# Layer 0's gate strips of six heads in pairs, by seven block products, ahead of attention 0

## The chip, the cores and the metric

One core of one Trainium2 chip runs the whole program in one launch. The metric is the device time of that core in microseconds (us), as the median over executions; lower is better. The engines are TensorE (PE, with its weight loads shown as PEld), VectorE (DVE), ScalarE (ACT), GpSimd (POOL) and SyncE (SP), which issues all the DMAs of this kernel.

## The reference, cut to what matters

A trunk of two layers on 1024 tokens of width 1024, all in float32. Each layer normalizes, applies a shift and a scale that come from a vector `c`, mixes the tokens, multiplies by a SiLU gate and projects back. Layer 0 is differential attention with eight heads; layer 1 is latent attention.

```python
def _diff_attention(h, positions, w_in, ...):
    proj = h @ w_in
    q, k, v, z = jnp.split(proj, [DA_WIDTH, 2 * DA_WIDTH, 3 * DA_WIDTH], axis=-1)
    q = _rope(q.reshape(b, s, 2 * DA_HEADS, DA_QK_DIM), positions)
    k = _rope(k.reshape(b, s, 2 * DA_HEADS, DA_QK_DIM), positions)
    ...
    def block(qb):
        sc = jnp.einsum('bqhcd,bkhcd->bhcqk', qb, k, preferred_element_type=f32) * scale
        p = jax.nn.softmax(sc, axis=-1)
        p = p[:, :, 0] - lam * p[:, :, 1]
        return jnp.einsum('bhqk,bkhd->bqhd', p.astype(v.dtype), v)
    o = _from_blocks(lax.map(block, _to_blocks(q)))
    o = _rmsnorm(o, subln_g) * (1.0 - lambda_init)
    o = o.reshape(b, s, DA_WIDTH) * jax.nn.silu(z)
    return o @ w_out
```

The change is about `z`, the gate: `h` (1024 x 1024) times the last 1024 columns of `w_in`. A head owns 128 of those columns; that is its gate strip.

## The kernel before, in words

**Numbers in two halves.** Every float32 operand of a matmul is split into a high part of PE's reduced format and the remainder. ACT writes the high part (a cast), POOL or DVE subtracts it from the raw value. `mm3` (L171 to L175) then makes a product of three matmuls: high by high, high by low, low by high. A strip (`strip0`, two raw tiles of 128x512 through `fetch_strip` and `split_raw`, L218 and L219) by 512 tokens is eight such products, 24 matmuls of 128x512; a whole strip is 48.

**Stages of layer 0, as PE runs them.** First the normalized, modulated and transposed tokens `h0[k][half]` are made (`h_chunk`) while the values of the heads 0 to 3 and part of the first key strip are multiplied. Then come the second halves of head 0's key and query strips (the `gen_half` loops ahead of `st1.close()`), then a stream of strips, of which `stream0.step(Z_PRE)` runs the first 16 steps (head 0's gate strip). A step is one `mm3`. Then `v0_tile` makes the values of heads 4 to 7, with weights `wv1`, and after that attention 0 runs head by head (`attn0`).

**Attention 0.** A head has eight query tiles. `q_tile` computes two score blocks per tile (c = 0 and 1, L866), each followed by a maximum on DVE (L412) and an exponential on ACT (L414); DVE combines both (L872 to L874). There are two score buffers in PSUM, so the second scores of a tile wait for the combination of the tile before. `after_scores` transposes the combined tile (L395), splits it (L397 on ACT, L398 on DVE) and, at every second tile, multiplies two tiles with the values (`pv`). Between these pieces the stream of strips is stepped: `FILL0` says how many steps at each of six places of a tile. Head by head the stream makes the key, query and gate strips of the next one. `side` is a list of small jobs (rotation and stacking of keys and queries), of which every step starts one.

**The order.** The program is traced in the order of the code; a planner then fixes each engine's order from its own costs: when an engine is free, it takes what is ready, earlier code first. `tc.issue_after(x)` puts a block's instructions behind x on x's engine; `in_turn` keeps program order. Buffers are named by pool and tag, with a fixed number each; a pool that is closed gives its space to the next one opened on the same side, and a new tile waits for the old tiles that lay there.

**Layer 1** already makes the gates of its heads 2 to 7 in pairs. `combos` forms sums and differences of the token blocks, `z_weights` those of the weight blocks, and `z_pair` combines seven products (`zacc` in the profile, L1801 to L1837); the finished gates go through DRAM (`zS`).

Of the kernel before, what the change touches and what calls it, by code (L numbers as in the profile page):

```python
# [21 lines left out]
P = 128  # L22
# [4 lines left out]
HF = 512  # L27
# [49 lines left out]
def f32v(ap):  # L77
    return ap.bitcast(F32)
# [3 lines left out]
def trunk(ctx: ExitStack, tc: tile.TileContext, A, out):  # L82
# [240 lines left out]

    def rope(rp, acc, half, scale, eng=G, add=V):

        cs = slice(half * HF, half * HF + HF)
        raw = rp.tile([P, HF], F32, name="rp_raw", tag="rp", bufs=6)
        sw = rp.tile([P, HF], F32, name="rp_sw", tag="rp", bufs=6)
        r = rp.tile([P, HF], F32, name="rp_r", tag="rp", bufs=6)
        if scale == 1.0:  # L330
# [212 lines left out]
    def load_wv(src, eng=G):  # L543
        return split_wv(fetch_wv(src), eng)
# [223 lines left out]
    def k_done(h):  # L768
        def f(acc, half):
            rot, fin = rope(wp, acc, half, 1.0, *[G if h else V] * 2)  # L770

# [10 lines left out]
    def q_done(h):  # L782
        def f(acc, half):
            rot, fin = rope(wp, acc, half, SC0, *[G if h else V] * 2)

# [24 lines left out]
    def strip0(kind, h):  # L810
        return lambda: fetch_strip([A["w_s0"][kind, h, f] for f in range(2)], [4, 4])

    items = []
    for h in range(NH):
        items += [(strip0(1, h), h0, k_done(h)), (strip0(0, h), h0, q_done(h)), (strip0(2, h), h0, z_done(h))]
    wv1 = [load_wv(A["w_v0"][k, 1], V) for k in range(WV1)]
    with tc.issue_after(mod_load.last):
        z0raw = fetch_strip([A["w_s0"][2, 0, f] for f in range(2)], [4, 4])
    with tc.issue_after(store_v.act):
        wv1 += [load_wv(A["w_v0"][k, 1], V) for k in range(WV1, KT)]  # L820
    with tc.issue_after(h_last):
        k_done(0)(kacc, 0)
    for _ in gen_half(wk0, h0, 1, lambda acc: k_done(0)(acc, 1)):
        pass
    wz0 = split_strip(z0raw)
    q_done(0)(qacc, 0)
    for _ in gen_half(wq0, h0, 1, lambda acc: q_done(0)(acc, 1)):
        pass
# [6 lines left out]
    stream0 = Stream(gen_strips(items[2:], [wz0]))  # L835
    lam4 = p1b.tile([P, 4, 64], F32, name="lam4", tag="lam", bufs=1)
    with tc.issue_after(mod_load.last):
        SP.dma_start(lam4, A["lam"].to_broadcast([P, 4, 64]))
    lp = sm.tile([P, 2], F32, name="lp")
# [38 lines left out]
    for tt in range(8):  # L878
# [6 lines left out]
        for t in pend[2 + 2 * tt : 4 + 2 * tt] if tt else ():  # L885
            with tc.issue_after(silu_gate.last):
                t()
# [268 lines left out]
    def gate_step0():  # L1156
        nonlocal slot0
        next(gate0, None)
        slot0 += 1

    for h in range(NH - 1):
        attn0(h, lambda i: FILL0[i], lambda i: gate_step0())
    class Seven:
# [627 lines left out]

    def gate_out(h, half, c_, dst):

        th = wst.tile([P, HF], F32, name="zth", tag="gz", bufs=3)
        S.activation(th, c_, AF.Tanh, scale=0.5)
        V.scalar_tensor_tensor(out=dst, in0=th, scalar=1.0, in1=c_, op0=ALU.add, op1=ALU.mult)
        SP.dma_start(zS[h, half], dst)

    zw = z_weights()
# [10 lines left out]
    def z_pair(p, late=lambda i: None):  # L1810
# [5 lines left out]
        V.tensor_add(c_, acc, u)  # L1816
        gate_out(2 * p, 0, c_, c_)
        V.tensor_add(u, product(TC[2]), u)
# [10 lines left out]
        V.tensor_add(u, acc, u)  # L1829
        gate_out(2 * p + 1, 1, c_, c_)  # L1830
# [4 lines left out]
        gate_out(2 * p + 1, 0, u3, u3)  # L1835
        V.tensor_add(u, product(h1q(1, 1)), u)
        gate_out(2 * p, 1, u, u)  # L1837

# [590 lines left out]
```

## Time and profile before

| what | us |
|---|---|
| median of three runs | 1400.3 |
| lowest and highest | 1397.07 and 1401.43 |
| the profiled execution's own time | 1398.53 |
| its span, first to last instruction | 1396.8 |
| PE busy | 1368.8 |
| DVE busy | 932.6 |
| ACT busy | 740.7 |
| POOL busy | 756.6 |
| mean granted clock of PE | 0.997 |

Busy times are of one profiled execution. Matmuls are pipelined, so the busy time of one (about 0.39 us for 128x512) is longer than the step from its start to the next one's.

### The profile page before, as it was taken

To read this page: it belongs to the slowest core of one execution; us is meant where nothing else is said; L and a number is where in the kernel's file an instruction comes from. 1 tells how busy PE (TensorE), PEld (TensorE's weight loads), DVE (VectorE), ACT (ScalarE), POOL (GpSimd) and SP (SyncE) were. 2 spreads that over 40 slices of the span, in tenths; PEclk is the share of its full clock that TensorE was granted. 3 is DMA by queue.
4 is the path that set the end of the run, shared out by engine and by line. 5 is a ranking of instruction groups with operands and counts; after the bars stand their busy time and mean duration, and the time that the engine had idled before them with its cause. 6 is when DMAs were issued, how large, how long until landed. Compare 5 with 4: busy or idle time off the path is not lost.

```text
span 1396.8 us, 20691 instructions
## 1 busy us (share of the span) xinstructions
PE 1368.8 (98%) x7334; PEld 1146.1 (82%) x7334; DVE 932.6 (67%) x1311; ACT 740.7 (53%) x1338; POOL 756.6 (54%) x592
## 2 busy tenths in 40 slices
PE   9999999999999999999999999999999999999997
PEld 6787888888888888887887888888888888888886
DVE  7654787777666666668596985645656555555684
ACT  5532465656555556566647552335454554545554
POOL 5434374758686858675794143532141273844673
PEclk9999999999999999999999999999999999999999
DMA  9857644343444434526555246399433364576463
GB/s 340 264 177 243 189 119 139 103 144 100 150 125 149 127 120 124 157 58 207 197 206 175 57 130 214 125 296 279 131 98 120 106 196 136 194 226 216 141 247 121
DMA packets 149386, 232.06 MB, mean 166 GB/s; under 512 B 20641, under 2 KB 57633, under 8 KB 149282
## 3 DMA queue, kind: packets, MB, share of 16 engines
q1 hardware_dynamic: 149282, 230.74, 52.2%
q8 instruction: 58, 0.95, 0.3%
q14 instruction: 46, 0.38, 0.1%
HBM read 144.74 MB, written 61.81 MB: 148 GB/s over the span
## 4 chain that ended last, share of the span: by engine, by line
PE 77%; DVE 7%; POOL 4%; DMA 4%; ACT 3%; issue 3%; SPq 1%; POOLq 0%; ACTq 0%; DVEq 0%
PE s L2043 10%; PE acc L173 8%; PE acc L175 8%; PE acc L174 8%; PE tr L395 7%; PE s L866 7%; PE pv L173 4%; PE pv L175 4%; PE pv L174 4%; DMA ada<-in_ada_ss 2%; PE oy L174 1%; PE oy L175 1%; PE oy L173 1%; DVE ada L436 1%; PE zacc L175 1%
## 5 line engine op out<-in xcount | busy, mean ns | idle before, releaser
L397 ACT CAST pth<-tr 128x512 fp32r<-128x512 f32 x256 | 150.3, 587 | 285.8 <-PE tr L395 281.2
L412 DVE TENSOR_REDUCE nm<-s 128x1 f32<-128x1024 f32 x192 | 234.0, 1219 | 78.7 <-PE s L866 70.5
L398 DVE TENSOR_TENSOR ptl<-tr,pth 128x512 fp32r<-128x512 f32 x256 | 176.3, 689 | 150.7 <-ACT pth L397 146.2
L219 POOL TENSOR_TENSOR wl<-wraw,wh 128x512 fp32r<-128x512 f32 (+2 forms) x77 | 102.3, 1330 | 211.9 <-ACT wh L218 168.8
L414 ACT ACTIVATE e<-s,nm 128x1024 f32<-128x1024 f32 x128 | 143.7, 1122 | 35.2 <-DVE nm L412 34.9
L395 PE MATMUL tr<-ident,e 128*128 128x128 f32 x1024 | 155.2, 274 | 4.0 <-DVE ptl L398 3.8
L395 PEld LDWEIGHTS tr<-ident,e 128*128 128x128 f32 x1024 | 120.7, 140 | 46.7 <-DVE ptl L398 24.5
L173 PE MATMUL acc<-h0h,wh 128*128 128x512 f32 x360 | 150.1, 417 | 0.0
L173 PE MATMUL pv<-pth,vt 128*128 128x256 f32 x512 | 147.6, 288 | 0.0
L174 PE MATMUL pv<-ptl,vt 128*128 128x256 f32 x512 | 145.5, 284 | 0.0
L175 PE MATMUL pv<-pth,vt 128*128 128x256 f32 x512 | 144.6, 282 | 0.0
L175 PE MATMUL acc<-h0h,wl 128*128 128x512 f32 x360 | 141.6, 393 | 0.0
L174 PE MATMUL acc<-h0l,wh 128*128 128x512 f32 x360 | 141.1, 392 | 0.0
L336 POOL TENSOR_TENSOR rp_r<-rp_raw,cosT 128x512 f32<-128x512 f32 x36 | 47.1, 1308 | 106.6 <-ACT rp_raw L333 53.2
L173 PEld LDWEIGHTS pv<-pth,vt 128*128 128x128 f32 x512 | 97.2, 190 | 2.9 <-ACT pth L397 0.2
L174 PEld LDWEIGHTS pv<-ptl,vt 128*128 128x128 f32 x512 | 97.4, 190 | 2.4
L175 PEld LDWEIGHTS pv<-pth,vt 128*128 128x128 f32 x512 | 97.3, 190 | 0.0
L1199 POOL TENSOR_TENSOR wol<-wol,woh 128x512 fp32r<-128x512 f32 x56 | 82.9, 1503 | 25.5 <-ACT woh L1198 23.9
L866 PE MATMUL s<-ks,qa 128*128 128x512 f32 x256 | 82.8, 404 | 4.2 <-DVE e L874 3.2
L874 DVE SCALAR_TENSOR_TENSOR e<-s,z,e 128x1024 f32<-128x1024 f32 x64 | 82.2, 1284 | 2.2
L866 PE MATMUL s<-ks,qb 128*128 128x512 f32 x256 | 79.9, 393 | 0.5 <-DMA qb<-qb 0.5
L175 PEld LDWEIGHTS acc<-h0h,wl 128*128 128x128 f32 x360 | 67.6, 188 | 15.0
(421 smaller groups left out, 3467.2 us busy)
## 6 DMA issues: line engine op xcount, KB each, us to landing
ada<-in_ada_ss SPq DMA_DIRECT2D x32, 512.0 KB, 5.7
wraw<-in_w_s SPq DMA_DIRECT2D x64, 256.0 KB, 2.8
vS<-v_hl SPq DMA_DIRECT2D x32, 512.0 KB, 5.7
vt<-vS SPq DMA_DIRECT2D x32, 512.0 KB, 4.8
wol<-tS SPq DMA_DIRECT2D x56, 256.0 KB, 5.3
tS<-ob SPq DMA_DIRECT2D x48, 256.0 KB, 2.0
rp_sw<-rp_raw SPq DMA_DIRECT2D x160, 64.0 KB, 2.0
bc_s<-bc_d SPq DMA_DIRECT2D x34, 256.0 KB, 3.9
```

The lines of the kernel that those rows point to most:

```text
L173: PE.matmul(psum, ah, bh, start=first, stop=False, skip_group_check=skip)
L174: PE.matmul(psum, ah, bl, start=False, stop=False, skip_group_check=skip)
L175: mm3.last = PE.matmul(psum, al, bh, start=False, stop=last, skip_group_check=skip).ins
L219: sub = (V if pair_of else G).tensor_sub(l_[:, :n], raw[:, :n], f32v(h_[:, :n]))
L395: transpose_p.last = PE.transpose(tr[:, j, :], p[:, kt * P : (kt + 1) * P], ident).ins
L397: mk["S"] = S.copy(pth[kh][:, :, dst], tr).ins
L398: mk["V"] = V.tensor_sub(ptl[kh][:, :, dst], tr, f32v(pth[kh][:, :, dst])).ins
L412: mk["V"] = V.reduce_max(nm, s_ps, axis=AX.X, negate=True).ins
L414: mk["S"] = S.activation(e, s_ps, AF.Exp, bias=nm, scale=1.0, accum_out=zs).ins
L866: PE.matmul(s_ps[:, kc * HF : (kc + 1) * HF], src[:, c, ql], KS[h][kc][:, c, :], start=fst, stop=not fst)
L1199: sub = eng.tensor_sub(lo, raw, f32v(hi))
L2043: PE.matmul(s_ps[:, kc * HF : (kc + 1) * HF], lhs, rhs(kc), start=i == 0, stop=i == 4)
```

## The change

Gate strips of layer 0's heads 0 to 5 are no longer made in attention 0's stream. They are made ahead of it, in three pairs. For a pair the two strips form a 2 x 2 block of weights (head by upper and lower half of the width, 512 rows each), the tokens a 2 x 2 block (width half by token half), and seven products of blocks, each four `mm3`, take the place of eight. Four of the seven take combinations of token blocks as their moving operand (`TK[1]` to `TK[4]`, made once by `combos0`, 17 jobs in `side`), and five take combinations of weight blocks (`z0_weights`). Head 6's gate strip is made whole ahead of the pairs, head 7's stays in the stream. All gates but head 7's are written to `zS` in DRAM and read back by `load_gates` at the second tile of their head.

To make room, the pools of the first stage (`p1a`, `p1b`) are closed earlier; the combinations live in their space (`zp` on the left, `tp` on the right). Head 0's keys and queries are written to DRAM as they come out of PSUM (`park`, `rS`) and are rotated later, from there. The query weights `wq0` move to pool `pg`. The value weights `wv1` are all loaded and split after the pairs. Head 1's key strip takes the 16 steps that head 0's gate strip had ahead of `v0_tile`. `FILL0` goes from 47 steps a head to 31, `Z_LAST` from 2 to 1.

The diff, cut to its core:

```diff
-FILL0 = ((1, 2, 1, 1, 1, 0), (1, 1, 1, 1, 1, 1)) * 3 + ((1, 2, 1, 1, 1, 0), (1, 1, 1, 1, 1, 0))
+FILL0 = ((1, 1, 1, 1, 1, 0), (1, 0, 1, 0, 1, 0)) * 3 + ((1, 1, 1, 1, 1, 0), (1, 0, 1, 0, 0, 0))
-Z_LAST = 2
-FILL7 = ((0, 1, 2, 1, 1, 0),) + ((0, 1, 1, 1, 1, 0),) * 2
+Z_LAST = 1
+Z_PAIRS = 3
+FILL7 = ((0, 1, 1, 1, 1, 0), (0, 1, 1, 1, 0, 0))
...
+    rS = dr.tile([2, 2, P, HF], F32, name="rS")
...
-    def rope(rp, acc, half, scale, eng=G, add=V):
+    def rope(rp, acc, half, scale, eng=G, add=V, parked=None):
...
+        src = raw if parked is None else parked
+        if parked is not None:
+            SP.dma_start(raw, parked)
...
-            SP.dma_start(sw[q * 32 : q * 32 + 32], raw[(q ^ 1) * 32 : (q ^ 1) * 32 + 32])
+            SP.dma_start(sw[q * 32 : q * 32 + 32], src[(q ^ 1) * 32 : (q ^ 1) * 32 + 32])
...
-        t = p1.tile([P, 2, HF], F32R, name="wq0", tag="ada", bufs=ADA_B)
+        t = pg.tile([P, 2, HF], F32R, name="wq0", tag="ada", bufs=2)
...
-        items += [(strip0(1, h), h0, k_done(h)), (strip0(0, h), h0, q_done(h)), (strip0(2, h), h0, z_done(h))]
-    wv1 = [load_wv(A["w_v0"][k, 1], V) for k in range(WV1)]
+        items += [(strip0(1, h), h0, k_done(h)), (strip0(0, h), h0, q_done(h))]
+    items.append((strip0(2, NH - 1), h0, z_done(NH - 1)))
...
+    def park(kind, scale):
+        def f(acc, half):
+            t = wp.tile([P, HF], F32, name="rp_park", tag="rp", bufs=6)
...
+            SP.dma_start(rS[kind, half], t)
+        return f
+
+    def gate_out(h, half, c_):
+
+        th = wst.tile([P, HF], F32, name="zth", tag="gz", bufs=3)
+        S.activation(th, c_, AF.Tanh, scale=0.5)
+        V.scalar_tensor_tensor(out=c_, in0=th, scalar=1.0, in1=c_, op0=ALU.add, op1=ALU.mult)
+        SP.dma_start(zS[h, half], c_)
...
     st1.close()
+    st1b.close()
+    stZ, stT0 = ExitStack(), ExitStack()
+    zp = pool(stZ, "zp")
+    tp = pool(stT0, "tp", side="right")
...
+    def combos0():
+        todo_ = []
+        def split_t():
+            n, k, t = todo_.pop(0)
+            hi, lo = TK[n][k] = [tp.tile([P, HF], F32R, name=f"t{n}{k}{x_}") for x_ in "hl"]
+            S.copy(hi, t)
+            V.tensor_sub(lo, t, f32v(hi))
+        def later(*job):
+            if todo_:
+                split_t()
+            todo_.append(job)
+        for k in range(4):
+            (ah, al), (bh, bl), (ch, cl), (dh, dl) = [[f32v(x_) for x_ in h0[k + 4 * q][half]] for half in range(2) for q in range(2)]
+            c_, d_, t1, t2, t3, t4 = [zt(x_) for x_ in ("tc", "td", "t1f", "t2f", "t3f", "t4f")]
+            V.tensor_add(c_, ch, cl)
+            V.tensor_sub(t1, c_, ah)
+            V.tensor_sub(t1, t1, al)
+            later(1, k, t1)
+            yield
+            V.tensor_add(d_, dh, dl)
+            V.tensor_sub(t2, d_, t1)
+            later(2, k, t2)
+            yield
+            V.tensor_sub(t4, bh, t2)
+            V.tensor_add(t4, t4, bl)
+            later(4, k, t4)
+            yield
+            V.tensor_sub(t3, d_, c_)
+            later(3, k, t3)
+            yield
+        split_t()
+        yield
+    def z0_weights():
+        for _ in range(Z_PAIRS):
+            a11, a12 = zraw[:2]
+            yield split_raw(a11, 4)
+            yield split_raw(a12, 4)
...
+            V.tensor_add(s1, a21, a22)
+            V.tensor_sub(a21, a11, a21)
+            V.tensor_sub(a11, s1, a11)
+            V.tensor_sub(a12, a12, a11)
+            for t in (a12, a11, s1, a21, a22):
+                yield split_raw(t, 4)
+    def product0(rhs):
+        hi, lo = zq.pop(0)
+        zq.append(next(zw, None))
+        acc = bank("acc", "zacc")
+        for k in range(4):
+            mm3(acc, hi[k], lo[k], *rhs[k], k == 0, k == 3)
+            side.tick()
+        return acc
+    def z0_pair(p):
+        u = rpt0("zu")
+        S.copy(u, product0(h0q(0, 0)))
+        c_ = rpt0("z11")
+        V.tensor_add(c_, product0(h0q(1, 0)), u)
+        gate_out(2 * p, 0, c_)
+        v = rpt0("zv")
+        S.copy(v, product0(h0q(1, 1)))
...
+        V.tensor_add(u, product0(TK[2]), u)
+        u5 = rpt0("zu5")
+        V.tensor_add(u5, product0(TK[1]), u)
+        V.tensor_add(v, v, u5)
+        gate_out(2 * p, 1, v)
...
+        acc = product0(TK[3])
+        V.tensor_add(u5, acc, u5)
+        V.tensor_add(u, acc, u)
+        gate_out(2 * p + 1, 1, u5)
+        V.tensor_add(u, product0(TK[4]), u)
+        gate_out(2 * p + 1, 0, u)
+    z0_fetch(0, ((0, 0), (0, 1), (1, 0), (1, 1)))
+    cg = combos0()
+    for _ in range(17):
+        side.add(lambda: next(cg), None)
+    for _ in gen_half(wk0, h0, 1, lambda acc: park(1, 1.0)(acc, 1)):
+        side.tick()
+    wz6 = split_strip(z6raw)
+    for _ in gen_half(wq0, h0, 1, lambda acc: park(0, SC0)(acc, 1)):
+        side.tick()
+    zw = z0_weights()
+    zq = [next(zw)]
+    for half in range(2):
...
+        for _ in gen_half(wz6, h0, half, put):
+            side.tick()
+    zq.append(next(zw))
+    for p in range(Z_PAIRS):
+        if p == Z_PAIRS - 1:
+            k1raw = fetch_strip([A["w_s0"][1, 1, f] for f in range(2)], [4, 4])
+        z0_pair(p)
+    stT0.close()
+    stZ.close()
...
+    wk1 = split_strip(k1raw)
+    for half in range(2):
+        k_done(0)(None, half, rS[1, half])
+    wv1 = [load_wv(A["w_v0"][k, 1], V) for k in range(KT)]
+    for half in range(2):
+        q_done(0)(None, half, rS[0, half])
+    stream0 = Stream(gen_strips(items[2:], [wk1]))
...
+    def beside0(h, i):
+        if i == 1:
+            load_gates(h)
+        gate_step0()
```

More of the change, by code (lines that the diff above doesn't have):

```diff
@@ L817, in trunk, with h0q @@
+    def gate_out(h, half, c_):
[3 more added lines that the diff above has]
+        SP.dma_start(zS[h, half], c_)
+    def h0q(q, half):
+        return [h0[4 * q + k][half] for k in range(4)]
     with tc.issue_after(mod_load.last):
[L818 to L820 removed]
+        z6raw = fetch_strip([A["w_s0"][2, NH - 2, f] for f in range(2)], [4, 4])
@@ L821, in trunk @@
     with tc.issue_after(h_last):
[L822 to L828, printed above, removed]
-    st1.close()
+        park(1, 1.0)(kacc, 0)
+    park(0, SC0)(qacc, 0)
+    st1.close()
+    st1b.close()
+    stZ, stT0 = ExitStack(), ExitStack()
+    zp = pool(stZ, "zp")
+    tp = pool(stT0, "tp", side="right")
+    TK = {n: [None] * 4 for n in range(1, 5)}
@@ new lines, in trunk, with z0_fetch, zt @@
+    zraw = []
+    def z0_fetch(p, parts):
+        for m, f in parts:
+            raw = zp.tile([P, HF], F32, name="zraw", tag="zraw", bufs=8)
+            SP.dma_start(raw, A["w_s0"][2, 2 * p + m, f])
+            zraw.append(raw)
+    def zt(name):
+        return zp.tile([P, HF], F32, name=name, tag="zt", bufs=8)
+    def combos0():
[30 more added lines that the diff above has]
+        yield
@@ L830, in trunk @@
+    zq.append(next(zw))
+    k1raw = None
+    for p in range(Z_PAIRS):
+        if p == Z_PAIRS - 1:
+            k1raw = fetch_strip([A["w_s0"][1, 1, f] for f in range(2)], [4, 4])
+        z0_pair(p)
+    assert not side.q and next(zw, None) is None
+    stT0.close()
+    stZ.close()
+    st1b = ExitStack()
+    p1b = pool(st1b, "p1c", side="right")
     st2a = ExitStack()
@@ L885, in trunk @@
         for t in pend[2 + 2 * tt : 4 + 2 * tt] if tt else ():
-            with tc.issue_after(silu_gate.last):
+            with tc.issue_after(split_wv.last):
                 t()
```

51 lines of the change are left out of this document (33 added, 18 removed).

## The prediction

> **What bounds the kernel now.** I read the page's head and chain first, then busy time by window, then single instructions around the places that the change touches.
>
> ```profile
> span 1396.8 us, 20691 instructions
> PE 1368.8 (98%) x7334; PEld 1146.1 (82%) x7334; DVE 932.6 (67%) x1311; ACT 740.7 (53%) x1338; POOL 756.6 (54%) x592
> PE 77%; DVE 7%; POOL 4%; DMA 4%; ACT 3%; issue 3%; SPq 1%; POOLq 0%; ACTq 0%; DVEq 0%
> ```
>
> PE is busy 98% of the span and 77% of the chain of waits runs through it. A matmul taken out is time won, unless another engine becomes late. By window (PE, PEld, DVE, ACT, POOL busy, granted clock, DMA share, GB/s):
>
> ```profile
> 81.20:92.20 11.00, 10.94 (x48) 9.08 (x49) 4.57 (x7) 3.45 (x7) 2.59 (x2) 1.00 0.95 275
> 92.20:103.10 10.90, 10.90 (x50) 9.03 (x49) 7.00 (x11) 4.45 (x8) 4.41 (x4) 1.00 0.42 118
> 148.00:640.00 492.00, 487.34 (x2716) 412.19 (x2715) 352.18 (x496) 290.19 (x514) 337.94 (x273) 1.00 0.43 127
> 859.00:916.90 57.90, 57.51 (x255) 47.29 (x254) 38.01 (x50) 21.01 (x37) 31.23 (x24) 1.00 0.53 175
> ```
>
> From 81.2 to 103.1 PE makes the second halves of head 0's key and query strips and then its gate strip, without a gap, while DVE has 11.6 of 21.9 us of work, most of it splits of `wv1` that move away. Attention 0 (148 to 640) is dense too. The window at 859 is layer 1's pair loop: the same seven products three times, also dense.
>
> **What is won.** Each pair saves one block product of 12 matmuls: 36 in all. Their pitch:
>
> ```profile
> 92.27 0.39 PE L173 MATMUL acc<-h0h,wh 128*128 128x512 f32 x1
> 103.15 0.39 PE L173 MATMUL vps<-wvh,h0h 128*128 128x512 f32 x1
> 859.07 0.39 PE L173 MATMUL zacc<-h_h,wh 128*128 128x512 f32 x1
> 916.88 0.39 PE L173 MATMUL vps<-wvh,ckh 128*128 128x512 f32 x1
> ```
>
> 48 matmuls take 10.88, so 0.227 each; 252 (three pairs of 84) take 57.81, or 0.229. 36 x 0.227 = **-8.2**. The rest only moves: 348 matmuls go ahead of `v0_tile` (48 + 3 x 84 + 48 for head 1's keys, in place of head 0's 48), 112 steps leave the seven heads.
>
> **The combined tokens and weights.** The new DVE work ahead of the first pair is 48 additions and subtractions of 128x512 (per k eight sums and four low parts). Four weight sums follow, and two gate multiplications of head 6 fall between. Their pitch is shown by layer 1's own combinations:
>
> ```profile
> 802.78 0.69 DVE L1628 TENSOR_TENSOR t4f<-h_h,t2f 128x512 f32<-128x512 f32 x1
> 807.60 0.69 DVE L1628 TENSOR_TENSOR t2f<-h1f,t1f 128x512 f32<-128x512 f32 x1
> 808.32 1.66 DVE L1628 TENSOR_TENSOR t4f<-h_h,t2f 128x512 f32<-128x512 f32 x1
> 807.41 2.02 POOL L219 TENSOR_TENSOR wl<-wraw,wh 128x512 fp32r<-128x512 f32 x1 [7.72 <-ACT wh L218]
> ```
>
> Eight instructions lie between the first two rows: 4.82/8 = 0.60 each. 48 take 29.0, well over the 21.9 of PE work that covers them.
>
> When can they start? The `zt` tiles lie where `p1a` was, and the values that wait for their store lay there last:
>
> ```profile
> 80.52 2.48 DVE L375 TENSOR_TENSOR v_hl<-vacc,v_hl 128x512 fp32r<-128x512 f32 x4
> 81.23 4.25 SPq L377 DMA_DIRECT2D vS<-v_hl  x4
> DMA to landing us min/median/max: 3.7/5.7/8.4
> ```
>
> The last stores go out between 81.2 and 85.5 and land 3.7 to 8.4 later. The earliest lands at 85, the last issued later; some buffers are free before others. I take 86.0; the limits are 83.0 (DVE's end of these values, if the space in question held others) and 87.
>
> When are they due? PE, dense, ends the key and query halves at 92.3 and head 6's strip at 103.15; the products follow each 12 x 0.227 = 2.73 apart: second 105.9, third 108.6, fourth 111.3. The third needs `a12'`, which is the last of the four weight sums. In code these sums are traced only when the first product is called, behind 47 of the 48 combinations (`side` puts an empty entry behind each job, so one job goes per two steps), and the planner takes earlier code first. Path: 86.0 + 29.0 = 115.0, + 2 gates and 4 sums at 0.6 = 118.6, then the split:
>
> ```profile
> L218 ACT CAST wh<-zraw 128x512 fp32r<-128x512 f32 x18 | 10.9, 618 | 16.6 <-PE zacc L174 9.7 <-DVE zraw L1787 3.6 <-POOL wl L219 1.5
> L219 POOL TENSOR_TENSOR wl<-zraw,wh 128x512 fp32r<-128x512 f32 x18 | 24.6, 1374 | 32.9 <-ACT wh L218 29.6 <-DVE zraw L1787 3.2
> ```
>
> 0.62 + 1.30 (the unhindered subtraction) = 120.5. The low part is first read at the third product's third matmul, 108.6 + 0.45 = 109.05. **+11.5** of PE idle. By then the fourth product's tokens are ready, and the later products' weights come from the same sums, two casts and subtractions per 2.73 us; nothing more is late in pair 1. In pairs 2 and 3 the layer 1 window, dense with the same work, says the weights are in time.
>
> The bounds of this term: with the start at 83.0 and the weights planned first, the last combination that the fourth product needs is ready at 83.0 + 46 x 0.604 + 2.4 = 113.2, due at 113.4 (its fourth k): **0**. With the start at 87 and three collisions like 808.32 (1.66 against 0.69, so 1.0 each): **15.6**. I take the middle of these paths, since the 80.52 and 81.23 rows put the start near 86 and nothing in the code puts the weights earlier.
>
> The Trainium skill, page "SBUF — State Buffer", section "Who interferes with whom", says that a VectorE instruction with both inputs in SBUF contends with a GpSimd instruction that reads SBUF, and that the loser waits. The 808.32 and 807.41 rows agree. By it all of the subtractions for head 6's strip and the first weights, some three in the window, would cost 1.0 each: the sum would be 3 higher. I keep them in the bound alone.
>
> **The clock behind the stall.** A long idle of PE lowered its granted clock at the head of layer 1:
>
> ```profile
> 767.08 0.33 PE L484 MATMUL trh<-ident,x 128*128 128x128 f32 x1 [2.85 <-DVE x L473]
> 760.00:770.00 10.00, 7.15 (x31) 5.46 (x30) 6.57 (x9) 5.36 (x9) 4.81 (x4) 0.89 0.30 102
> 770.00:780.00 10.00, 10.00 (x52) 8.22 (x52) 8.74 (x12) 5.27 (x9) 0.00 (x0) 0.94 0.07 16
> ```
>
> 0.11 x 10 + 0.06 x 10 = **+1.7**, once; 0 without the stall.
>
> **Attention 0 with less to fill.** Each tile pair loses four steps of stream. Between the second scores of a tile and the combination that frees the buffer runs a chain on DVE and ACT (columns as above: start, duration):
>
> ```profile
> 311.76 0.62 PE L866 MATMUL s<-ks,qa 128*128 128x512 f32 x2
> 316.24 1.28 DVE L874 SCALAR_TENSOR_TENSOR e<-s,z,e 128x1024 f32<-128x1024 f32 x1
> 317.93 0.62 PE L866 MATMUL s<-ks,qa 128*128 128x512 f32 x2
> 336.18 0.73 PE L866 MATMUL s<-ks,qa 128*128 128x512 f32 x2 [0.55 <-DVE e L874]
> ```
>
> The chain is 317.52 - 311.76 = 5.76, PE's own work over the same path 6.17. One step less (3 x 0.23 = 0.69) makes 5.48: short by 0.28. The pair at 336.18, where DVE also does the normalization's row, waits already (0.55) and would be short by up to 0.68 more. With 28 pairs, 14 of each kind, nothing moved: 14 x 0.27 + 14 x 0.68 = 13.3. But the planner draws matmuls of the stream forward when the scores aren't ready:
>
> ```profile
> 282.77 1.28 DVE L874 SCALAR_TENSOR_TENSOR e<-s,z,e 128x1024 f32<-128x1024 f32 x1
> 283.78 0.39 PE L173 MATMUL acc<-h0h,wh 128*128 128x512 f32 x1
> 284.24 0.63 PE L866 MATMUL s<-ks,qa 128*128 128x512 f32 x2
> ```
>
> There two of the next step's three matmuls stand ahead of the scores, which could start at 284.05. So most of the shortage can be covered from steps nearby: I take **+2.0**, from 0 to 4.9 (14 x 0.27 plus 1.1), and 13.3 as a rival. DVE (352 of 492) and POOL (338 of 492) have room; they lose the gates' work and gain nothing but POOL's share of keys and queries that they had.
>
> **Values, DMAs, queue.** All eight `wv1` loads now start when the combined tokens' space is free, 8.2 us before the pairs end, through two raw buffers:
>
> ```profile
> wvr<-in_w_v SPq DMA_DIRECT2D x20, 256.0 KB, 5.0
> ```
>
> Four rounds of two at 5.0 us, less overlap, against a need 10.9 to 15.7 us behind the pairs (head 1's keys, 48 matmuls, then the first values): late by 0 to 3, **+1.0**. The new transfers (four writes and twenty reads for parked keys and queries, fourteen stores and loads of gates at 256 KB) meet a DMA share of 0.43 in attention, and the gates are loaded a tile ahead; SP issues are small beside that: 0. The DMA share of 0.95 at 81.2 falls off by 92 and the first pair's four weight loads are due at 103. `Z_LAST` starts the out-projection's loads one tile earlier: **-0.5** (0 to -1.5; PE idles 3.9 in the window below).
>
> ```profile
> 640.00:690.00 50.00, 46.10 (x274) 37.89 (x273) 35.31 (x55) 32.18 (x58) 32.90 (x28) 1.00 0.56 181
> ```
>
> **Sum.** -8.2 + 11.5 + 1.7 + 2.0 + 1.0 - 0.5 = **+7.5** on the profiled execution's 1398.53 = 1406.0. That execution is 1.8 under the median of 1400.3; I halve the difference and say **1407**. All terms at their low ends, -8.2 - 1.5 = -9.7, give 1390.6 on the median; at their high ends, -8.2 + 15.6 + 1.7 + 4.9 + 3.0 = +17.0, give 1417.
>
> **Rivals.**
> - *A, the forecast, 0.42:* weight sums late, PE waits about 11 us at the third product. For it: code order and 29 us of sums against 21.9 of cover.
> - *B, the other side, 0.30:* the sums are in time. Place: DVE before the third product; price 0 to 2; it decides if the start is near 83 and the planner draws the weight sums ahead of the tokens that aren't needed until the fourth product. For it: matmuls were drawn forward at 283.78, so order is not bound to the code. Then -8.2 + 1 + 2.0 + 1.0 - 0.5 = -4.7, and -8.2 if attention loses nothing: 1392 to 1396.
> - *C, 0.20:* the weights go early but the start is 86, so the fourth product waits for `T2`: 86 + 29 + 2.4 = 117.4 against 113.4, +4.0 and 1.7 of clock. -8.2 + 5.7 + 2.5 = 0: 1399 to 1401.
> - *D, 0.08:* attention's chain of scores becomes the bound, 13.3 in place of 2.0. With the first stall hidden -8.2 + 13.3 + 0.5 = +5.6, 1405; with it 1418.
>
> That the change doesn't do what it says can be left out: layer 1's pairs run at 0.229 a matmul.
>
> **How the numbers follow.** What a measurement of this kernel can tell from no change is about 0.3%, 4.2 us. A is slower by its 6.7, D too with most of its weight; B is faster beyond the limit for most of its part, C the same. With A's lower edge (a stall of 7) and B's upper in the middle: faster 0.30, same 0.24, slower 0.46. A's own range is 1402 to 1413; since both signs have weight, the range goes from B's lower bound to A's upper, 1391 to 1416.
>
> **What would show it.** An idle stretch of PE ahead of the third product of the first pair, released by DVE's weight sums or POOL's subtraction behind them, some 11 us long, with a granted clock under 1 behind it; first combination near 86; pairs at 57.3 without more waits; the first seven heads of attention each 16 x 0.69 = 11 us shorter, with no wait of the scores for the combination beyond 0.3; values waiting under 3 us for `wvl`. I am wrong if PE is dense from 81 to 160, or if the weight sums stand ahead of the combinations on DVE.

## The result and the profile after

The changed kernel takes 1438.2 us (median of 4, 1436.5 to 1440.3) against 1399.2: 1.0279 of the time before, 95% interval 1.0256 to 1.0303, 39 us slower. The direction was the likeliest of three in the forecast (slower 0.46), the size was not forecast: 1407 with a range up to 1416. The page after:

```profile
span 1437.3 us, 20898 instructions
PE 1373.7 (96%) x7298; PEld 1141.9 (79%) x7298; DVE 986.8 (69%) x1392; ACT 760.2 (53%) x1369; POOL 773.2 (54%) x601
PE 60%; DVE 6%; ACT 3%; DMA 2%; issue 1%; POOL 1%; SPq 0%; POOLq 0%; ACTq 0%; DVEq 0%
```

36 matmuls are gone (7334 to 7298), as counted. PE's busy time still rises by 5 us, in part because matmuls at half clock are longer, and its share falls to 96%.

To see where 39 us went, the program is cut at the same places in both traces: the first product of the pairs, the first values, the first scores of the heads 1 and 7, the first product of the out-projection. On PE before (start, duration, ...) these are, beside the first values at 103.15:

```profile
206.37 0.40 PE L866 MATMUL s<-ks,qa 128*128 128x512 f32 x1
620.60 0.40 PE L866 MATMUL s<-ks,qa 128*128 128x512 f32 x1
653.80 0.50 PE L173 MATMUL oy<-woh,oah 128*128 128x512 f32 x1
```

and after:

```profile
103.12 0.39 PE L175 MATMUL zacc<-h0h,wh 128*128 128x512 f32 x1
180.11 0.39 PE L175 MATMUL acc<-h0h,wh 128*128 128x512 f32 x1
190.99 0.39 PE L175 MATMUL vps<-wvh,h0h 128*128 128x512 f32 x1
295.19 0.40 PE L1026 MATMUL s<-ks,qa 128*128 128x512 f32 x1
660.29 0.40 PE L1026 MATMUL s<-ks,qa 128*128 128x512 f32 x1
694.77 0.50 PE L175 MATMUL oy<-woh,oah 128*128 128x512 f32 x1
```

| stage, after | us | its matmuls without a wait | lost |
|---|---|---|---|
| three pairs | 77.0 | 252 x 0.2275 = 57.3 | 19.7 |
| head 1's keys | 10.9 | 10.9 | 0 |
| values and head 0 | 104.2 | 94.0 (the run without combinations, below) | 10.2 |
| heads 1 to 6 | 365.1 | 414.2 (before) - 296 x 0.2275 = 346.9 | 18.2 |
| head 7 to the out-projection | 34.5 | 33.2 (before) - 3 x 0.2275 = 32.5 | 2.0 |

Six heads at 48 matmuls each would be 288 less, but the traces have 846 matmuls of the stream there before and 550 after: eight now run earlier, beside head 0. (Some expectations below count 288 and so put this loss at 16.) Lost 50.1, won 8.2: 41.9. The two spans differ by 40.5: PE of the kernel before also waits, for 1.1 us, among its values, and 0.5 is won from the out-projection on. Up to the pairs (103.12 against 103.15) nothing moved.

**The pairs.** Instructions on PE, then on DVE and POOL, columns as in the prediction:

```profile
109.97 0.50 PE L177 MATMUL zacc<-h0h,wl 128*128 128x512 f32 x1 [3.52 <-POOL wl L221]
125.01 0.79 PE L175 MATMUL zacc<-h0h,wh 128*128 128x512 f32 x1 [11.24 <-ACT wh L220]
```

```profile
84.65 0.69 DVE L883 TENSOR_TENSOR tc<-h0h,h0l 128x512 f32<-128x512 f32 x1 [1.77 <-DMA vS<-v_hl]
90.53 0.69 DVE L884 TENSOR_TENSOR t1f<-tc,h0h 128x512 f32<-128x512 f32 x1 [5.19 <-DMA vS<-v_hl]
117.01 0.68 DVE L911 TENSOR_TENSOR zs<-zraw 128x512 f32<-128x512 f32 x1
123.63 0.68 DVE L914 TENSOR_TENSOR zraw<-zraw 128x512 f32<-128x512 f32 x1
103.42 6.50 POOL L221 TENSOR_TENSOR wl<-zraw,wh 128x512 fp32r<-128x512 f32 x1 [9.03 <-ACT wh L220]
```

The first combination starts at 84.65 and the second at 90.53: one stored value has landed, the next has not. From there DVE is full to 124.3, the end of the last weight sum; the four sums are spread over its last 7 us. PE waits 11.24 us for the cast behind the last of them. A smaller wait of 3.52 stands before it: the subtraction for the second product took 6.50 us on POOL in place of 1.3. Behind both, the clock (windows as in the prediction, the last three numbers granted clock, DMA share, GB/s):

```profile
111.00:114.40 3.40, 2.77 (x7) 1.65 (x5) 3.40 (x7) 1.34 (x3) 0.00 (x0) 0.50 0.62 227
117.80:125.00 7.20, 0.00 (x0) 0.00 (x0) 7.11 (x12) 2.50 (x5) 0.00 (x0) 0.50 0.00 1
125.00:131.40 6.40, 6.25 (x14) 4.48 (x15) 2.20 (x3) 2.25 (x5) 4.19 (x3) 0.50 0.40 124
```

At half clock PE does six matmuls in 2.8 us, from 111.0 until the long wait begins (the seventh of the row began earlier), and fourteen in 6.4: 20 in 9.2, which is 4.6 more than 20 x 0.2275. Waits and clock, 3.5 + 11.2 + 4.6 = 19.3, are the loss of 19.7 but for 0.4; at each wait the last matmul also ends later than the next one would have started. Pairs 2 and 3 have no wait.

**The values.** The first load of `wv1` goes out 7.3 us after the pairs end, and PE waits in the first value tile and again for the buffers of stored values; in the whole stretch (the last row, a window) it idles for 7.5 us:

```profile
187.38 0.84 SPq L545 DMA_DIRECT2D wvr<-in_w_v  x2
194.69 0.73 PE L175 MATMUL vps<-wvh,h0h 128*128 128x512 f32 x2 [1.82 <-ACT wvh L554]
213.87 0.50 PE L175 MATMUL vps<-wvh,h0h 128*128 128x512 f32 x1 [2.37 <-DVE v_hl L380]
190.99:295.19 104.20, 96.70 (x475) 77.60 (x474) 73.22 (x107) 49.07 (x87) 50.77 (x38) 1.00 0.66 204
```

**Attention.** PE's waits from head 0 to head 6 (waiting, releaser, us, times, longest), before and after:

```profile
PE s L866 <- DVE e L874: 1.9, 4, 0.7
```

```profile
PE s L1026 <- DVE e L1034: 9.4, 8, 4.8
```

Head by head (first scores to first scores) it isn't spread over all pairs of tiles. The second row counts the matmuls of the stream that are gone, the third takes them off at 0.2275 us each:

| head | 1 | 2 | 3 | 4 | 5 | 6 |
|---|---|---|---|---|---|---|
| before | 67.8 | 68.5 | 68.8 | 69.9 | 70.2 | 69.1 |
| matmuls gone | 40 | 64 | 48 | 48 | 48 | 48 |
| before less these | 58.7 | 53.9 | 57.9 | 59.0 | 59.3 | 58.2 |
| after | 63.4 | 61.9 | 57.6 | 65.4 | 58.8 | 57.9 |

Heads 3, 5 and 6 lost nothing. In head 4 one event makes most of it:

```profile
489.52 2.45 SPq L340 DMA_DIRECT2D rp_sw<-rp_raw  x4
493.66 1.29 POOL L346 TENSOR_TENSOR rp_sw<-rp_sw,sinT 128x512 f32<-128x512 f32 x1 [2.09 <-DMA rp_sw<-rp_raw]
496.32 0.62 ACT L361 CAST ks<-rp_r 64x512 fp32r<-64x512 f32 x1 [6.33 <-POOL rp_r L348]
499.93 1.10 PE L1026 MATMUL s<-ks,qa 128*128 128x512 f32 x2 [4.77 <-DVE e L1034]
500.10:503.50 3.40, 3.40 (x10) 2.62 (x11) 2.73 (x3) 2.49 (x5) 2.76 (x3) 0.50 0.41 120
```

A key's rotation lands at 493.4. ACT's cast of that key, needed only by the next head, stands ahead of the exponential in ACT's row; ACT waits 6.33 for it; the exponential, the combination and the scores wait behind. The 3.4 us after this wait run at a granted clock of 0.50; wait and clock together are about the 6.4 that this head lost. In head 2 PE waits 2.2 us in all for the stream's own weights (`wh` and `wl`) and 1.4 for a combination, and 3.4 us there run at half clock too. The 4.7 us of head 1 have no single wait above 0.7.

### The profile page after: what moved, and what is told of

It is laid out like the page before. It is cut to its first block, busy times and chain, and to the rows that moved or that the text cites. A ratio compares the mean times of both kernels' runs of the same rounds, so it can differ in the third digit from the quotient of the medians.

```text
span 1437.3 us, 20898 instructions
## 1 busy us (share of the span) xinstructions
PE 1373.7 (96%) x7298; PEld 1141.9 (79%) x7298; DVE 986.8 (69%) x1392; ACT 760.2 (53%) x1369; POOL 773.2 (54%) x601
## 4 chain that ended last, share of the span: by engine, by line
PE 60%; DVE 6%; ACT 3%; DMA 2%; issue 1%; POOL 1%; SPq 0%; POOLq 0%; ACTq 0%; DVEq 0%
PE s L2206 10%; PE tr L400 6%; PE acc L177 5%; PE acc L176 5%; PE s L1026 5%; PE acc L175 5%; PE pv L175 3%; PE pv L177 3%; PE pv L176 3%; PE oy L175 1%; PE oy L176 1%; PE oy L177 1%; PE zacc L177 1%; PE zacc L175 1%; PE zacc L176 1%
## 5 line engine op out<-in xcount | busy, mean ns | idle before, releaser
L417 DVE TENSOR_REDUCE nm<-s 128x1 f32<-128x1024 f32 x192 | 233.6, 1217 | 18.5 <-PE s L1026 9.2
L221 POOL TENSOR_TENSOR wl<-wraw,wh 128x512 fp32r<-128x512 f32 (+2 forms) x65 | 83.9, 1292 | 204.4 <-ACT wh L220 155.0
L419 ACT ACTIVATE e<-s,nm 128x1024 f32<-128x1024 f32 x128 | 143.5, 1121 | 58.8 <-DVE nm L417 58.6
L176 PE MATMUL pv<-ptl,vt 128*128 128x256 f32 x512 | 148.5, 290 | 0.7 <-DVE ptl L403 0.7
L175 PE MATMUL acc<-h0h,wh 128*128 128x512 f32 x264 | 108.8, 412 | 0.8 <-ACT wh L220 0.7
L177 PE MATMUL acc<-h0h,wl 128*128 128x512 f32 x264 | 104.5, 396 | 1.8 <-POOL wl L221 1.8
L176 PE MATMUL acc<-h0l,wh 128*128 128x512 f32 x264 | 104.2, 395 | 0.0
L221 POOL TENSOR_TENSOR wl<-zraw,wh 128x512 fp32r<-128x512 f32 (+2 forms) x39 | 56.8, 1461 | 85.5 <-ACT wh L220 82.2
L1026 PE MATMUL s<-ks,qa 128*128 128x512 f32 x256 | 86.0, 416 | 12.9 <-DVE e L1034 10.7
L1026 PE MATMUL s<-ks,qb 128*128 128x512 f32 x256 | 83.7, 401 | 0.0
```

Of the source, the lines that this page charges most:

```text
L175: PE.matmul(psum, ah, bh, start=first, stop=False, skip_group_check=skip)
L176: PE.matmul(psum, ah, bl, start=False, stop=False, skip_group_check=skip)
L177: mm3.last = PE.matmul(psum, al, bh, start=False, stop=last, skip_group_check=skip).ins
L221: sub = (V if pair_of else G).tensor_sub(l_[:, :n], raw[:, :n], f32v(h_[:, :n]))
L417: mk["V"] = V.reduce_max(nm, s_ps, axis=AX.X, negate=True).ins
L419: mk["S"] = S.activation(e, s_ps, AF.Exp, bias=nm, scale=1.0, accum_out=zs).ins
```

## The experiments

All are edits of the changed kernel unless said. "Values" is from the first values to head 1's first scores; times are medians of four executions or more, against the changed kernel's 1438.2. The kernel before, run beside them, had medians from 1399.1 to 1400.7, so 1 to 2 us between two runs say little. Each edit also lets the planner set every order anew, and not only at the edited place.

**1. The weight sums first.** They are written to new tiles, ahead of the combinations.

```diff
...
+    w_first.append(zraw[:2])
+    w_sums.append(z0_sums())
     cg = combos0()
```

> The changed kernel with one thing moved: the four weight sums of the first pair stand ahead of the token combinations in the code (they write new tiles instead of overwriting raw ones). Order theory (the pair's third product waits because its weight sums stand at the end of VectorE's row): the idle of 11.2 us ahead of the third product is gone; the fourth product then waits for the last t2 (90.5 + 49 x 0.603 = 120.1 against 116.8, about 4 us), the half-clock stretch is shorter; time 8 to 11 us below the changed kernel, so about 1428. Total theory (VectorE's 56 instructions from 90.5 on are the bound in any order): the idle only moves to the fourth product and stays over 8 us; gain under 4 us.

1435.9, ratio to the kernel before 1.0258 [1.0243, 1.0273]: 2.3 us gained. The wait at the third product is gone, and came back elsewhere:

```profile
117.47 0.49 PE L175 MATMUL zacc<-t22h,wh 128*128 128x512 f32 x1 [2.90 <-ACT t22h L872]
141.15 0.50 PE L175 MATMUL zacc<-h0h,wh 128*128 128x512 f32 x1 [2.01 <-ACT wh L220]
```

The pairs take 74.8 instead of 77.0. Of the two the total theory is nearer: the gain is under 4 us. But the idle doesn't stand at the fourth product as it said; eight waits of 2.9 us at most make 10.5, where it was 14.8, and with the clock the pairs still lose 17.5. The order on DVE chooses which products wait, and changes little in what the pairs lose. The prediction's rival with the weights ahead (4 us of stall and 1.7 of clock) falls with it.

**2. No combinations.** The later products multiply plain tokens.

```diff
-    for _ in range(17):
-        side.add(lambda: next(cg), None)
+    for n in TK:
+        TK[n] = [h0[k + 4 * (n % 2)][n // 2 % 2] for k in range(4)]
```

> The changed kernel without the 48 token combinations; products 4 to 7 of each pair multiply plain token blocks, so the first six gates are not the reference's. Token theory (VectorE's combinations delay everything in the pair stage, the weight sums behind them and the subtraction on GpSimd beside them): the pairs run dense at 57.3 us, the half clock behind them is gone, 19 to 21 us below the changed kernel, about 1418, with the values and attention as they were. Rival (the weights' own path of cast and subtraction is too slow for the first pair): the third product still waits over 5 us, gain under 14 us.

1414.8 [1.0089, 1.0123], 23.4 gained, more than either theory gave: the pairs fell by only 13.5, and the values by 10.2.

```profile
88.76 0.62 SPq L545 DMA_DIRECT2D wvr<-in_w_v  x1
...
113.79 0.33 SPq L545 DMA_DIRECT2D wvr<-in_w_v  x1
103.50:167.00 63.50, 59.12 (x253) 46.78 (x253) 50.44 (x66) 23.86 (x43) 33.13 (x22) 1.00 0.51 174
177.90:271.90 94.00, 94.00 (x475) 78.12 (x474) 53.36 (x76) 43.75 (x77) 46.50 (x36) 1.00 0.53 151
```

Without combined tokens their space is empty, so the eight `wv1` loads go out from 88.8 to 113.8 and their splits run on DVE beside the pairs; the values then run dense. Two causes were taken away at once, and the next run parts them.

**3. Cheap combinations.** The same tiles, held as long, by one cast and one subtraction each.

```diff
...
+                hi, lo = TK[n][k] = [tp.tile([P, HF], F32R, name=f"t{n}{k}{z_}") for z_ in "hl"]
+                S.copy(hi, x_)
+                V.tensor_sub(lo, x_, y_)
```

> The changed kernel with the combined tokens' tiles filled as before, but by one cast and one subtraction each from plain token tiles (16 instructions on VectorE in place of 64 with their splits), so the first six gates are not the reference's. It tells VectorE's time from the space: the tiles are still held to the end of the pairs. Space theory (the 10 us that the values lost came back without combinations only because the wv1 loads found free space): pairs as without combinations (63.5 us), but values to head 1 still near 104 us; about 1424. Rival (the values were late because VectorE and GpSimd were late out of the pairs): values to head 1 near 94 us, about 1415.

1419.7 [1.0131, 1.0161], 18.5 gained. The pairs are dense, 57.1 us, the values stay at 105.5:

```profile
81.00:103.20 22.20, 22.20 (x99) 18.39 (x99) 15.24 (x24) 14.44 (x25) 6.51 (x3) 1.00 0.73 221
103.20:120.00 16.80, 16.80 (x75) 13.92 (x75) 8.56 (x10) 6.26 (x12) 7.99 (x6) 1.00 0.33 99
```

So the 19.7 us of the pairs come from DVE's additional instructions. There are 48, 32 sums and 16 low parts (the expectation's 64 is a miscount); the edit takes away the sums, and with them the tiles that waited until 90.53 for stored values, so how many instructions and how late a start can't be told apart here: without the sums the low parts begin at 86.58 and end at 96.3. The values' 10 us are there as long as the space is held: the first load goes out at 167.8, again 7 us after the pairs. In both runs heads 1 to 6 still take 364 to 366 us: attention lost its time for another reason.

**4. More cover: two pairs.** Heads 6, 5 and 4 whole, then two pairs.

```diff
-Z_PAIRS = 3
+Z_PAIRS = 2
...
+    Stream(gen_strips([(strip0(2, h), h0, put(h)) for h in range(NH - 2, 2 * Z_PAIRS - 1, -1)], [wz6])).step(99)
```

> The changed kernel with two pairs in place of three: the gate strips of heads 6, 5 and 4 are made whole, one after another, ahead of the pairs. 12 more matmuls (2.7 us), and 21.8 us more of PE work while VectorE makes the combinations. Cover theory (PE waits in the first pair only since 34 us of VectorE have 12 to 18 us of matmuls beside them): no idle over 1 us in the pairs, no half clock, 2.7 - 17 to 20 = 14 to 17 us below the changed kernel, about 1422. Rival (the subtractions on GpSimd beside a busy VectorE, or the weights, hold the first pair wherever it stands): 0 to 5 us gain.

1427.2 [1.0184, 1.0218], 11.0 gained in spite of 12 more matmuls.

```profile
103.00:129.00 26.00, 23.64 (x97) 19.08 (x96) 24.50 (x36) 10.34 (x18) 12.08 (x5) 0.93 0.34 102
129.00:167.10 38.10, 38.10 (x169) 31.55 (x168) 18.28 (x24) 14.72 (x25) 18.62 (x14) 1.00 0.20 67
```

The pairs are dense; one wait of 2.37 for POOL's subtraction now stands in a whole strip, with 3.4 us at half clock behind it (the 0.93), so the first product starts 4.1 us later than 21.8 us of matmuls would put it. That is all that is left of the 19.7. The cover theory holds for the pairs; its gain of 14 to 17 left this wait out.

**5 and 6. The values' loads earlier.** First the eight loads ahead of the parked keys in the code (5); then also four raw buffers (6).

```diff
     wk1 = split_strip(k1raw)
+    wv1 = [load_wv(A["w_v0"][k, 1], V) for k in range(KT)]
     for half in range(2):
         k_done(0)(None, half, rS[1, half])
-    wv1 = [load_wv(A["w_v0"][k, 1], V) for k in range(KT)]
```

> The changed kernel with the eight wv1 loads ahead of head 0's parked keys in the code. Queue theory (the loads stand behind the reads of parked keys on SP, which wait for buffers of the pairs' results, so the first goes out at 187.4, 7 us after the pairs' end): first load before 180, no wait of the values for wvh or wvl, time 3 to 6 us below the changed kernel. Space theory (the loads wait for the combined tokens' space): first load stays near 187, no gain.

> The changed kernel with the wv1 loads ahead of the parked keys in the code and four raw buffers in place of two. Buffer theory (with two raw buffers a load waits for the cast and subtraction before it, 4.2 us per two): the eight loads go out within 9 us, the values wait under 1 us for wvh and wvl, 4 to 8 us below the changed kernel, about 1432. Rival (the order on SP decides: what gains for the values is lost for parked keys and stored values behind them, as when the loads alone were moved): 1438 to 1446.

Neither helped: 1445.5 [1.0315, 1.0345] and 1440.5 [1.0281, 1.0313]. In the fifth the first load goes out at 183.6, between the two theories: on SP it now stands behind a store of the pairs' gates. In the sixth the waits for weights are down to 0.5 us, and the loss stands at the stores of finished values:

```profile
206.75 7.05 SPq L340 DMA_DIRECT2D rp_sw<-rp_raw  x5
220.47 0.66 SPq L382 DMA_DIRECT2D vS<-v_hl  x1
226.72 0.58 ACT L379 CAST v_hl<-vps 128x512 fp32r<-128x512 f32 x1 [11.06 <-DMA vS<-v_hl]
228.08 0.50 PE L175 MATMUL vps<-wvh,h0h 128*128 128x512 f32 x1 [3.62 <-DVE v_hl L380]
```

The first tiles were ready at 202 to 216; SP sends the first at 220.47, behind rotations that wait for their source and behind other loads. By these rows, what is gained for the weights is lost to the row on SP.

**7 and 8. Is it the number of SP's issues?** One transfer per rotation in place of four (rows not swapped), in the changed kernel and, as a control, in the kernel before.

```diff
-        for q in range(4):
-            SP.dma_start(sw[q * 32 : q * 32 + 32], src[(q ^ 1) * 32 : (q ^ 1) * 32 + 32])
+        SP.dma_start(sw, src)
```

> The changed kernel with the rotation's swapped copy made by one transfer of 128 rows in place of four of 32 (the rows are not swapped, so keys and queries are not the reference's): 108 issues fewer on SP. SP theory (values and attention lose about 26 us because the issues of the rotations, close together and in order, hold the stores and loads behind them): values to head 1 from 104 to under 99 us, heads 1 to 6 from 365 to under 358 us, total 12 to 18 us below the changed kernel. Rival (it is the landing time and the order that was planned for, not the number of issues): within 4 us of the changed kernel.

> The kernel before with the same edit to the rotation (keys and queries are not the reference's). SP theory: there the rotations are spread over the gate strips and nothing waits behind them, so within 2 us of the kernel before; if it gains as much as the changed kernel does, the issues are no matter of the change.

1446.8 [1.0302, 1.0342], and 1404.2 [1.0013, 1.0034] for the kernel before. Values 102.5, heads 1 to 6 367.2. The SP theory in this form falls: taking issues away made both kernels slower, by 8.6 and 3.5 us, more than either theory allowed. Why is not shown; the planner's new orders may be the reason. That what counts is the waits in a row that is kept in order is argued from the rows of run 6, not shown by a run of its own.

**9. Gates not read back.** A resident table in their place.

```diff
...
-            SP.dma_start(GZ[h][half], zS[h, half])
+        GZ[h] = [cosT[:, half * HF : half * HF + HF] for half in range(2)]
```

> The changed kernel, but attention multiplies by a resident table in place of the gates read back from DRAM, so 14 loads of 256 KB leave SP and the transfers; the gates are not the reference's. Gates' transfer theory (heads 1, 2 and 4 are 4 to 7 us longer than their matmuls because the gate loads delay the rotation's transfers): heads 1 to 6 fall from 365 to under 355 us, about 1427. Rival (keys and queries follow each other with no gate strip between, so rotations and weight splits come closer together, whatever DRAM does): heads 1 to 6 stay at 362 to 366, time within 3 us of the changed kernel.

1439.9 [1.0270, 1.0301], heads 1 to 6 at 366.2. The loads of the gates have no part in attention's loss.

**10. The fill moved.** The same steps a head, two at the even tiles' second place again.

```diff
-FILL0 = ((1, 1, 1, 1, 1, 0), (1, 0, 1, 0, 1, 0)) * 3 + ((1, 1, 1, 1, 1, 0), (1, 0, 1, 0, 0, 0))
+FILL0 = ((1, 2, 1, 1, 1, 0), (1, 0, 1, 0, 0, 0)) * 3 + ((1, 2, 1, 1, 1, 0), (1, 0, 0, 0, 0, 0))
```

> The changed kernel with the same 31 steps a head, placed otherwise: the even query tiles keep the two steps at the second place that they had before (1,2,1,1,1,0) and the odd tiles lose one more (1,0,1,0,0,0). Chain theory (attention lost 16 us because PE's own work between a tile's second scores and the combination fell under the 5.76 us of VectorE and ScalarE): waits of the scores for the combination fall from 9.4 us to about 2, time 7 to 10 us below the changed kernel, about 1430. Rival (attention lost it to late weights, late keys and the clock, or to too few steps wherever they stand): within 3 us of the changed kernel.

1450.7 [1.0352, 1.0383], 12.5 slower. Heads 1 to 6 take 63.4, 58.7, 65.7, 57.7, 66.5 and 61.7: others lose now. The waits for the combination in these heads are 10.3 us, where the chain theory said about 2. That theory falls; the gap it should have filled wasn't the cause.

**11. The strips shifted by eight steps.** 8 steps of head 1's keys ahead of the values, 32 a head, 8 in head 7.

```diff
-FILL0 = ((1, 1, 1, 1, 1, 0), (1, 0, 1, 0, 1, 0)) * 3 + ((1, 1, 1, 1, 1, 0), (1, 0, 1, 0, 0, 0))
+FILL0 = ((1, 1, 1, 1, 1, 0), (1, 0, 1, 0, 1, 0)) * 4
...
-Z_PRE = 16
+Z_PRE = 8
...
-FILL7 = ((0, 1, 1, 1, 1, 0), (0, 1, 1, 1, 0, 0))
+FILL7 = ((0, 1, 1, 1, 1, 0), (0, 1, 1, 1, 1, 0))
```

> The changed kernel with 8 steps of head 1's key strip ahead of the values in place of 16, 32 steps a head in place of 31, and the eight left over in head 7, so that every strip comes 8 to 2 steps later in its head. Phase theory (heads 1, 2 and 4 lose 16 us because the stacking of a head's second queries waits for the last tile of the head before and then meets the rotation of the next keys): heads 1 to 6, whose matmuls take 348.7 + 6 x 0.68 = 352.8 us, come to 353 to 358 us in place of 365; total 1428 to 1434, since the values have less ahead of them. Rival (the place of the strips doesn't matter): 366 to 372 us, total 1438 to 1446.

1436.5 [1.0243, 1.0273]. The heads take 59.4, 58.6, 60.1, 62.4, 59.7 and 58.6, 358.8 in all with 18 matmuls more (4.1 us): the loss there is 7.8 in place of 18.2. The time didn't follow, since the values now have less ahead of them: 4.5 us of waiting for `wvh` ahead of the first one, 6.8 us at half clock about its end, and 109.7 us of values in place of 104.2. That attention's loss depends on where keys and queries fall among the tiles is shown. That each case is a cast ahead of the exponential, as in head 4, isn't: of PE's waits for the combination in these heads, 9.4 us in the changed kernel, most remain, only each is shorter:

```profile
PE s L1026 <- DVE e L1034: 7.4, 11, 2.2
```

**12. Three together.** Two pairs, the shift, the early loads with four buffers.

> The changed kernel with three of the single edits together: two pairs in place of three, the strips' place shifted by eight steps, and the wv1 loads early with four raw buffers. If the causes stand for themselves: two pairs -11, the shift -1.7 and, since its 4.7 us of waiting for wvh is what the early loads take away, up to another -5: about 1421, heads 1 to 6 near 359 us. If the shift only moved the loss from attention to the values, it stays at 1425 to 1428. Either way it is not below the kernel before.

1417.3 [1.0114, 1.0148], 20.9 gained, where the single edits add up to 10.5 (11.0, 1.7 and a loss of 2.2): pairs dense (38.1), heads 1 to 6 at 359.1, values at 102.6 where the shift alone had 109.7. So the loss wasn't only moved from attention to the values. The early loads, no help by themselves, seem to pay once the shift needs them; no run has these two alone. It is the best of the versions that still compute the reference's result, and 18 us slower than the kernel before.

**13. The out-projection's loads alone.** The kernel before with `Z_LAST` and `FILL7` of the change.

```diff
-Z_LAST = 2
-FILL7 = ((0, 1, 2, 1, 1, 0),) + ((0, 1, 1, 1, 1, 0),) * 2
+Z_LAST = 1
+FILL7 = ((0, 1, 1, 1, 1, 0), (0, 1, 1, 1, 0, 0))
```

> The kernel before with the out-projection's loads one tile earlier and the last seven steps of the stream in two tiles of head 7 (Z_LAST 1 and FILL7 as in the change) and nothing else. The prediction's term: 0.5 us less, from 0 to 1.5 less. Rival: head 7 up to the out-projection is longer, as in the changed kernel (34.5 us against 33.2), about 1 us more.

1401.8 [1.0008, 1.0027], 2.4 slower. Head 7 takes 35.5 instead of 33.2, with as many matmuls of the stream. What the stream has left when the loads begin runs at once: six steps, 18 matmuls, in one block at 634.25. In the kernel before, four of them lie between the pieces of the third tile. A new wait stands behind that tile, which now has none:

```profile
645.06 0.66 PE L395 MATMUL tr<-ident,e 128*128 128x128 f32 x4 [1.30 <-DVE ptl L398]
```

## Why the prediction was right in part and wrong in size

| term | forecast | measured |
|---|---|---|
| matmuls saved | -8.2 | -8.2 |
| first pair, waits and clock | +13.2 | +19.7 |
| attention, heads 1 to 6 | +2.0 | +18.2 |
| values | +1.0 | +10.2 |
| `Z_LAST` | -0.5 | +2.0 (all of head 7) |

**The first pair: the mechanism was right, its size too small.** PE waited at the third product for the weight sums behind the combinations, with the clock down behind it. That this wait is 11.2 us against 11.5 forecast is luck: both its ends lie some 5 us later than forecast. What was mis-sized: the start was taken as one time, 86.0, where the first tile came free at 84.65 and the others at 90.53. The last weight sum ended at 124.3, not 118.6. The collision of POOL and DVE was priced on DVE (1.0 each, kept in the bound alone); here it mostly hit POOL, 6.50 against 1.3, and cost 3.5 us at the second product. With the half clock behind it, that moved the third product later. The clock was taken as 1.7 from the dip at 767; two stretches of 3.4 and 13.7 us at half clock cost 4.6. The bound of 15.6 for the stall held with waits of 14.8, and only the clock put this term above its high end.

**The values: the step that failed is "all eight loads start when the combined tokens' space is free, 8.2 us before the pairs end".** The first went out at 187.4, 7.3 us after the end, and at 183.6 when nothing of the parked keys stood ahead of it in the code. The term was put at 1.0 and measured 10.2. The prediction put SP's row at 0 ("SP issues are small beside that"). Fewer issues don't help, as run 7 shows; that the waits of a row kept in order are the cost is what the rows of run 6 say.

**Attention: the step that failed is to cost it by the chain of scores alone, with "most of the shortage" covered from steps nearby: +2.0, and 18.2 measured.** Rival D gave 13.3 if nothing were filled, not far from 18.2, but that would have been luck: three heads of six lost nothing, and fill put back into the chain's gap made it worse. What the forecast didn't cost is that a head's gate strip was 16 steps in which no rotation or stacking is due; without it keys and queries follow each other, and run 11 shows that 10 of the 18 us depend on where they fall among the tiles. "DVE and POOL have room" was true of their sums, and no help to an instruction behind another in its row. The event itself is shown for head 4 alone; for heads 1 and 2 the cause stays open.

**`Z_LAST`: the sign was wrong.** Of the 3.9 us of idle in the window 640 to 690 only 0.8 stands ahead of the out-projection's matmuls; 2.8 are waits of the attention. Taking the steps out of head 7's third tile adds one more.

The other side (in time, 0.30) is excluded by the trace, the half stall (0.20) by run 1: DVE's work doesn't fit, in either order. The upper end of the range, 1416, is called A's upper end, which the same text gives as 1413, and the sum of all high ends as 1417; no choice among these would have held 1438.

A rule of the Trainium skill bears on the collision: the page "SBUF — State Buffer", section "Who interferes with whom", says that the engine that issues first keeps the shared ports for its instruction and the other one is blocked. It names VectorE instructions with two inputs in SBUF, against GpSimd ones that read SBUF. The rows in the last section agree: in its 6.50 us POOL came through only beside the gate's multiplication, whose second input lies in PSUM.

## What to carry to other kernels

Work that is moved ahead needs its cover counted on the engine that prepares it: 34 us of additions, begun 18 us ahead of the product that needed the last of them, stalled in both orders tried, and only more matmuls between, or fewer additions, helped. Space that is held for a stage also dates the loads of the stage behind it, and in a row kept in order, what stands behind a late transfer waits with it. A filler stream is more than its length: the same steps at another place of the head were worth 10 us of attention here, so a part taken out should be tried at several phases before its saving is counted.

## What the runs showed of the hardware

A wholly idle PE isn't needed for the clock to fall. In run 5 (values early) three short waits of 0.39, 0.22 and 1.00 us were followed by 6.8 us at half clock:

```profile
193.00:196.10 3.10, 1.50 (x5) 0.48 (x3) 0.70 (x2) 1.23 (x2) 1.61 (x1) 1.00 0.68 215
196.10:199.50 3.40, 3.38 (x6) 1.91 (x7) 1.38 (x2) 0.62 (x1) 0.00 (x0) 0.50 0.57 169
```

PE made five matmuls in 3.1 us, and the next six at half clock. In head 2 of the changed kernel a stretch with 2.10 us of busy PE was followed by half clock too:

```profile
360.00:363.60 3.60, 2.10 (x8) 1.11 (x8) 2.51 (x5) 2.45 (x5) 3.45 (x4) 0.99 0.72 199
363.60:367.00 3.40, 3.40 (x12) 2.71 (x11) 0.94 (x1) 0.00 (x0) 3.32 (x3) 0.50 0.55 154
```

The stretches at half clock in all these runs last 3.4 us or a multiple of it, apart from the one that the end of an execution cuts. So in run 5 three waits of 1.6 us in all cost up to 3.4 in clock, half of the 6.8.

A subtraction on GpSimd of 1.3 us took 6.50, from 103.42 to 109.92 in the changed kernel, beside an unbroken row on VectorE of which these are the first and the last three:

```profile
103.89 0.68 DVE L893 TENSOR_TENSOR t4f<-t4f,h0l 128x512 f32<-128x512 f32 x1
...
108.11 0.67 DVE L888 TENSOR_TENSOR td<-h0h,h0l 128x512 f32<-128x512 f32 x1
108.72 0.67 DVE L807 SCALAR_TENSOR_TENSOR gz<-zth,acc 128x512 f32<-128x512 f32 x1
109.31 1.15 DVE L889 TENSOR_TENSOR t2f<-td,t1f 128x512 f32<-128x512 f32 x1
```

Its own 1.3 us fit at its end, from 108.6 on, where VectorE reads `acc` and so one input less from SBUF; the next addition is delayed by 0.5. Two engines that each have time to spare can still stop each other.
